# A two-layer hybrid trunk on one core: first token tile ahead of the norm scales, GpSimd makes the first weights' low part, squares added ahead of their sums, meta tokens' sums sent first

## Chip, core and metric

The kernel runs on one core of a Trainium2 chip. The metric is the device time of one execution in microseconds (us), lower is better. A profiled execution gives a trace beside it: a record for each instruction of TensorE (PE, with its weight loads as PEld), VectorE (DVE), ScalarE (ACT) and GpSimd (POOL), the issues of transfers by SyncE (SP), and the packets of the transfers.

## What is computed

Two layers over 528 tokens, 16 learned meta tokens ahead of 512, with a residual stream of 1024 channels. Each layer normalises the stream, projects it once into all inputs of two mixers (a causal pooling mixer, and latent attention with a rotary part and normalised queries and keys), gates both and adds the result:

```python
for l in range(DEPTH):
    h = rmsnorm(h_res, norm_gain[l])
    proj = h @ w_in[l]
    u_pool, z_pool, c_q, c_kv, k_rope, z_mla, g_pool, g_mla = jnp.split(proj, IN_SPLIT_POINTS, axis=-1)
    y_pool = (pool_mix(u_pool, pool_w_group[l], pool_scale[l]) * jax.nn.silu(z_pool)) @ pool_w_up[l]
    o_mla = mla(c_q, c_kv, k_rope, pos, ...)
    y_mla = (o_mla * jax.nn.silu(z_mla)) @ mla_w_up[l]
    merged = jax.nn.sigmoid(g_pool) * y_pool + jax.nn.sigmoid(g_mla) * y_mla
    h_res = h_res + merged @ w_out[l]
return h_res[:, N_META:]
```

Inside `mla` the latents `c_q` (768 wide) and `c_kv` (256 wide) have norms of their own; `q` and `k` of each of 8 heads (64 channels without and 32 with rotation) are normalised over their 96 channels. All in float32.

## The kernel before, in words

**Layout and products.** Activations lie transposed, channels on the 128 partitions and 528 tokens along the free axis. The stream is in eight tiles `xb[0..7]`, 128 channels each. Every big product is three products of the faster format fp32r: each operand is split into a high and a low part, and `mm3` adds high x high (L205), high x low (L206) and low x high (L207) in one accumulator. Weights come in pieces of 128x512: `wload` takes the piece, ScalarE writes its high part (L200), VectorE the low part (L201). The stream's tiles are split in the same way, scaled by the layer's gain: `hh` by ScalarE (L371), `hl` by VectorE (L373). The row of 528 tokens is cut in two halves of 264 (`FULL`), since an accumulator holds 512.

**What sets the order.** `plan` lists the projections with their columns and their `evac`, the code that reads an accumulator when it is complete. `stream` walks the plan, loads each weight piece some steps ahead and yields a nominal time after each few products; `step` takes one such piece of work. The rest of the kernel (norm statistics, attention heads) is straight code that asks for filler between its parts: `fill_now(ns)` runs steps worth so many nominal ns, `fill` does so up to a due time (`FILL`), and `after(ns, fn)` runs `fn` when so much filler has passed (`BACK`, `LATE`). From the code written in this way a scheduler fixes each engine's instructions in one static order. `behind(a, b)` makes `a` wait for `b`, and `follow(a, b)` only orders them. Transfers are nearly all issued by SP, in its order.

**The start.** The first weight piece is loaded by ScalarE's queue (tile `rinv`), then SP issues the gains (`gn`), the first token tile `xb[0]`, a second weight piece and `xb[1]`. `first` is the load of `gn`; all other loads of the start (`other_loads`) wait for it. The low and high part of the first two pieces lie in wide tiles `th`. GpSimd meanwhile clears some tiles. TensorE multiplies nine tiles of ones (L157) until the first operands are there; its first real products read `hh`, `hl` and `th` into `S`.

**Norm statistics.** `square_x` has ScalarE square the tiles of the stream and GpSimd add them to pairs and to fours: two tiles remain (of layer 1; layer 0 takes the sums from row copies of the input instead). `row_sums`, for layer 0, loads the tokens by rows (`xrow`, and `mrow` for the meta tokens), in nine pieces; ScalarE squares each and adds along the row into `sx`. `norm_sums` runs products with a block of ones (L426) over the two tiles of the stream and the two tiles `csq` of squares of `c_kv`, 32 columns wide, side by side in the array by `tile_position`; it writes the sums to `nsr` in DRAM (L440, and from `sx` L404 and L405), reads them back in another shape (`nq`, L448), and VectorE computes the inverse roots (`newton`) for `rinv` and the scale of `c_kv`, by which every accumulator of the projections is scaled when it is read.

**Statistics of queries and keys.** `q_stat` squares each block of the queries as it leaves its accumulator: two blocks `r` with the rotary channels of four heads each, four blocks `p` with the other channels of two heads each. `stat` collects the squares, `stat_go` sends a product (L535) for each of them, in two halves, with a matrix of constants that selects the heads, and `qk_stats` follows with the inverse roots.

**Heads.** `head` computes scores, exponentials and their row sums `rs`; the blocks go out to DRAM (`pdr`) and return transposed to `attE`, in `back`, some filler later. The inverse row sums go by DRAM (`rdr`) to a broadcast `rb`, and `gate` multiplies them into the gate on GpSimd.

Of the kernel before, what the change touches and what calls it, by code (L numbers as in the profile page):

```python
# [27 lines left out]
H = 8  # L28
# [3 lines left out]
TWO_PI = 2.0 * math.pi  # L32
SWAP = [i ^ 16 for i in range(32)]
# [19 lines left out]
FILL = (2620.0, 2530.0)  # L53
# [27 lines left out]
def trunk(ctx, tc, xT, xrow, mrow, pos, win, wkr, wqb, wkb, wvb, wgr, wpu, wmu, wout, gains, const, yT):  # L81
# [60 lines left out]
    act.dma_start(early[0][:, 0:512], win[0, MT_CKV, :, 0:512])  # L142
    first = sp.dma_start(gn, gains)
    sp.dma_start(xb[:, 0, :T], xT[:, 0, :])
# [45 lines left out]
    loads = [0]  # L190

    def wload(src, n, spare, home=None):
        raw = early.pop(0) if early else fetch(src, n, rawt() if home is None else home, sp)
        loads[0] += 1
        if loads[0] <= 2 or spare:
            t = wide()
            hi, lo = t[:, 0:512], t[:, 512:1024]
        else:
            hi, lo = (wp.tile([P, 512], F32R, tag=t, name=nm(t), bufs=3) for t in ("whi", "wlo"))
        act.activation(hi[:, :n], raw[:, :n], AF.Copy)  # L200
        dve.tensor_sub(lo[:, :n], raw[:, :n], hi[:, :n].bitcast(F32))  # L201
        return hi, lo
# [135 lines left out]
    nsr = [dp.tile([4, T], F32, name=f"nsr{l}") for l in range(DEPTH)]  # L338
# [9 lines left out]
    class Layer:  # L348
        def __init__(self, l):
# [11 lines left out]
            self.sq, self.half = [], halves()  # L361
# [14 lines left out]
        def square_x(self, k):  # L376
            self.xsq[k] = slot(f"cq{4 + k}" if k < 4 else f"q{k}")
            made = act.activation(self.xsq[k][:, :T], self.xt[k][:, :T], AF.Square)
            for w in (1, 2):
# [4 lines left out]
        def row_sums(self):  # L384
            sx = sm.tile([P, 2, 5], F32, tag="sx", name=nm("sx"))
            tags = ("q4", "q5", "q6", "q7", "kn0", "kn1", "kn2", "bc", "bc")
            rows = []
            for i in range(2 * len(tags) + 4):
# [3 lines left out]
                if i % 2 == 0 and len(rows) < len(tags):  # L392
                    k = len(rows)
                    r, src = (P, xrow[:, k]) if k < 8 else (2 * NM, mrow)
                    rows.append(slot(tags[k], bufs=3 if tags[k] == "bc" else 1)[0:r, 0:512])
                    behind(sp.dma_start(rows[k], src), newest[0])
                if i % 2 == 1 and i >= 5:
                    k = (i - 5) // 2
                    t = rows[k]
                    made = act.activation(t, t, AF.Square, accum_out=sx[0:t.shape[0], k % 2, k // 2:k // 2 + 1])  # L400
                    behind(made, newest[0])
                yield
            raw = nsr[0]
            sp.dma_start(raw[0:2, NM:T].rearrange("h (p i) -> p h i", i=4), sx[:, :, 0:4])  # L404
            sp.dma_start(raw[0:2, 0:NM].rearrange("h m -> m h"), sx[0:2 * NM, 0, 4:5])  # L405

        def norm_sums(self):
# [10 lines left out]
            px, pc = mmt() if self.l else None, mmt()  # L418
            xs = self.xsq[::4] if self.l else []
            runs = [(px, t, m, m < 2, m >= len(xs) - 2) for m, t in enumerate(xs)]  # L420
            runs += [(pc, t, m, True, True) for m, t in enumerate(self.csq)]
            for k in range(0, len(runs), 2):
                for s, (a, b) in enumerate(FULL):
                    for ps, t, m, start, stop in runs[k:k + 2]:
                        g = 64 * s + 32 * (m % 2)
                        mm = pe.matmul(ps[g:g + 32, :HALF], ones[:, 0:32], t[:, a:b], start=start, stop=stop,  # L426
                                       tile_position=(0, g))
                        if t is not self.csq[1]:
                            behind(mm, self.csq_last)
            self.kr_sums()  # L430
            sums = tmp()
            for s, (a, b) in enumerate(FULL):
                if self.l:
                    act.activation(sums[0:64, a:b], px[64 * s:64 * s + 64, :HALF], AF.Copy)
                dve.tensor_copy(sums[64:128, a:b], pc[64 * s:64 * s + 64, :HALF])
            raw, norms = nsr[self.l], ndr[self.l]
            if self.l:
                sp.dma_start(raw, sums[0:97:32, 0:T])
            else:
                sp.dma_start(raw[2:4], sums[64:97:32, 0:T])  # L440
                for _ in rows:
# [4 lines left out]
            nq = sm.tile([16, 4, C], F32, tag="nq", name=nm("nq"))  # L446
# [3 lines left out]
            dve.scalar_tensor_tensor(out=na[:, 0, :], in0=nq[:, 1, :], scalar=1.0 / D, in1=na[:, 0, :],  # L450
                                     op0=ALU.mult, op1=ALU.add)
            dve.tensor_scalar(na[:, 1, :], na[:, 0, :], EPS, None, op0=ALU.mult)
            dve.tensor_scalar(ny[:, 2, :], na[:, 1, :], EPS, None, op0=ALU.mult)
            for m in range(2):
# [841 lines left out]
```

## Time and profile before

| | us |
|---|---|
| median of three runs | 756.11 |
| the runs | 755.23 to 756.22 |
| the profiled execution | 756.64 |
| its span, from the first to the last instruction | 754.9 |
| TensorE busy in it | 749.7 |
| VectorE, ScalarE, GpSimd busy | 548.1, 395.9, 218.8 |

The profiled execution lies 1.74 us above its own span; that part, ahead of and behind the instructions, has no records. A row of the timeline gives start and duration in us, engine, line, operation, written tile <- read tiles, shape and, in brackets, how long the engine had been idle before and what released it. Rows with an engine's name and a q are of its sequencer (issues of transfers, configuration). A row of the chain gives start, duration, engine, tile and line of a stretch on the chain that ended last. A row of waits gives the waiting line, what it waited for, and us in total, times, and the longest.

### The profile page before, as it was taken

Reading aid. Unit: us, or ns where it says so; the run is one execution under the profiler, and the core shown is the slowest. Engines: PE = TensorE matmul, PEld = TensorE weight load, DVE = VectorE, ACT = ScalarE, POOL = GpSimd, SP = SyncE. Lnnn points to the kernel's source line nnn. Section 1 sums busy time; section 2 is a strip of 40 time slices with the busy share of each in tenths; the row PEclk is TensorE's granted clock in tenths of the full one; section 3 lists DMA queues with packets and bytes.
Section 4 is the critical chain, followed back from the end, with each engine's and each line's share of the span. In section 5 each row is a group of like instructions: output and inputs, shape, how many; then the busy total and the mean of one; then the engine's idle time right before and its main releaser. Section 6 shows DMA issues by size and latency. Waiting matters only on the chain.

```text
span 754.9 us, 14329 instructions
## 1 busy us (share of the span) xinstructions
PE 749.7 (99%) x5038; PEld 682.9 (90%) x5038; DVE 548.1 (73%) x1209; ACT 395.9 (52%) x866; POOL 218.8 (29%) x267
## 2 busy tenths in 40 slices
PE   9999999999999999999999999999999999999998
PEld 8999899999999999999997898887788888888887
DVE  5588777457999988684466477676478999975942
ACT  6755655645565665542355446456345666653321
POOL 1126404204463620061130264023044435111400
PEclk9999999999999999999999999999999999999999
DMA  8532223443765567525642322234447756773472
GB/s 316 162 108 89 74 82 86 113 116 119 211 186 166 151 194 192 156 86 157 183 145 85 114 84 66 89 90 120 108 135 210 190 156 181 195 200 93 127 227 84
DMA packets 72853, 106.58 MB, mean 141 GB/s; under 512 B 14102, under 2 KB 34966, under 8 KB 72780
## 3 DMA queue, kind: packets, MB, share of 16 engines
q1 hardware_dynamic: 72636, 105.39, 47.6%
q8 instruction: 40, 0.66, 0.4%
q14 instruction: 33, 0.27, 0.1%
q10 hardware_dynamic: 144, 0.26, 0.1%
HBM read 89.76 MB, written 15.86 MB: 140 GB/s over the span
## 4 chain that ended last, share of the span: by engine, by line
PE 98%; DMA 1%; ACT 0%; SPq 0%; issue 0%; DVE 0%; ACTq 0%
PE mm L205 29%; PE mm L207 29%; PE mm L206 29%; PE S L205 2%; PE S L207 2%; PE S L206 2%; PE o L980 1%; PE o L983 1%; PE S L535 1%; PE S L881 1%; DMA attE<-pdr 1%; PE S L501 0%; DMA xb<-xT 0%; PE mm L995 0%; PE mm L426 0%
## 5 line engine op out<-in xcount | busy, mean ns | idle before, releaser
L205 PE MATMUL mm<-hh,whi 128*128 128x264 f32 (+2 forms) x1072 | 336.1, 315 | 0.6 <-ACT whi L200 0.6
L206 PE MATMUL mm<-hl,whi 128*128 128x264 f32 (+2 forms) x1072 | 336.6, 315 | 0.0
L207 PE MATMUL mm<-hh,wlo 128*128 128x264 f32 (+2 forms) x1072 | 336.4, 316 | 0.0
L201 DVE TENSOR_TENSOR wlo<-raw,whi 128x512 fp32r<-128x512 f32 (+2 forms) x238 | 173.4, 730 | 95.8 <-ACT whi L200 92.4
L200 ACT ACTIVATE whi<-raw 128x512 fp32r<-128x512 f32 (+2 forms) x238 | 142.3, 600 | 176.1 <-PE mm L206 136.4
L205 PEld LDWEIGHTS mm<-hh,whi 128*128 128x128 f32 x1072 | 201.3, 188 | 15.0 <-issue 0.8
L206 PEld LDWEIGHTS mm<-hl,whi 128*128 128x128 f32 x1072 | 201.6, 188 | 12.9
L207 PEld LDWEIGHTS mm<-hh,wlo 128*128 128x128 f32 x1072 | 200.9, 188 | 12.3
L649 POOL TENSOR_TENSOR racc<-racc,tmp 128x264 f32<-128x264 f32 (+1 forms) x15 | 14.4, 959 | 132.3 <-ACT tmp L648 132.3
L1055 POOL TENSOR_TENSOR tmp<-tmp,xb 128x264 f32<-128x264 f32 (+1 forms) x24 | 27.0, 1137 | 49.1 <-DVE tmp L1053 46.4
L833 DVE CUSTOM_DVE_ANT_0 S<-S,maskw,nqs 128x240 f32<-128x240 f32 (+4 forms) x80 | 37.8, 492 | 4.2 <-PE S L207 3.9
L811 POOL CAST qhl<-q 32x528 fp32r<-32x528 f32 (+1 forms) x32 | 25.1, 800 | 44.2 <-PE S L881 42.9
L809 POOL CAST kh<-cq 32x528 fp32r<-32x528 f32 x16 | 15.6, 976 | 69.8 <-issue 36.1
L206 PE MATMUL mm<-th,whi 128*128 128x264 f32 (+1 forms) x108 | 34.7, 321 | 0.0
L205 PE MATMUL mm<-cq,whi 128*128 128x264 f32 (+1 forms) x108 | 34.7, 321 | 0.0
L205 PE MATMUL mm<-u,whi 128*128 128x264 f32 (+1 forms) x108 | 34.6, 321 | 0.0
L206 PE MATMUL mm<-cq,whi 128*128 128x264 f32 (+1 forms) x108 | 34.5, 321 | 0.0
L207 PE MATMUL mm<-cq,wlo 128*128 128x264 f32 (+1 forms) x108 | 34.5, 321 | 0.0
L207 PE MATMUL mm<-u,wlo 128*128 128x264 f32 (+1 forms) x108 | 34.5, 319 | 0.0
L959 DVE TENSOR_TENSOR attE<-attE,th 128x640 fp32r<-128x640 f32 x32 | 26.9, 862 | 3.7 <-ACT th L958 3.7
L840 ACT ACTIVATE cq<-S,bia 128x400 f32<-128x400 f32 (+2 forms) x48 | 24.4, 511 | 9.2 <-DVE bia L894 7.7
L843 POOL COPY pm<-cq 128x16 f32<-128x16 f32 x32 | 18.2, 570 | 37.7 <-ACT cq L840 37.5
(301 smaller groups left out, 1369.5 us busy)
## 6 DMA issues: line engine op xcount, KB each, us to landing
raw<-win SPq DMA_DIRECT2D x143, 256.0 KB, 3.2
pdr<-attD SPq DMA_DIRECT2D x16, 640.0 KB, 3.7
attE<-pdr SPq DMA_DIRECT2D x64, 160.0 KB, 3.9
raw<-wout SPq DMA_DIRECT2D x32, 256.0 KB, 2.8
raw<-wpu SPq DMA_DIRECT2D x16, 256.0 KB, 2.7
raw<-wmu SPq DMA_DIRECT2D x16, 256.0 KB, 2.7
raw<-wqb SPq DMA_DIRECT2D x12, 256.0 KB, 2.6
xb<-xT SPq DMA_DIRECT2D x8, 264.0 KB, 5.5
```

Source lines behind the costliest of these rows:

```text
L200: act.activation(hi[:, :n], raw[:, :n], AF.Copy)
L201: dve.tensor_sub(lo[:, :n], raw[:, :n], hi[:, :n].bitcast(F32))
L205: first = pe.matmul(out, wh, xh, start=start, stop=False)
L206: pe.matmul(out, wh, xl, start=False, stop=False)
L207: newest[0] = pe.matmul(out, wl, xh, start=False, stop=stop)
L809: gp.tensor_copy(d[r0:r0 + 32, :], f[g0:g0 + 32, :])
L811: gp.tensor_copy(d[r0:r0 + 32, x0:T], f[g0:g0 + 32, x0:T])
L833: return dve.tensor_tensor_reduce(out=sv, in0=sv, in1=mask, scale=nqs[:, i, h:h + 1], scalar=3e38, op0=ALU.add, op1=ALU.min, accum_out=bia ...
L840: act.activation(pv, sv, AF.Exp, scale=-1.0, bias=bia[:, i:i + 1], accum_out=rs[:, c:c + 1])
L843: gp.tensor_copy(pm[:, i, 16 * odd:16 * odd + 16], pt[i][:, 0:NM])
L959: dve.tensor_sub(got[:, a:b], f[:, a:b], hi[:, a:b].bitcast(F32))
L1055: gp.tensor_add(t[:, :b - a], t[:, :b - a], self.am[m][:, a:b])
```

## The change

In the order of the code:

- `SEAT` gives the heads of one rotary block another order, so that the rotary squares of two heads lie on the partitions on which the squares of their other channels are added.
- SP issues `xb[0]` ahead of `gn`. The other loads of the start still wait for `gn`.
- `wload` has the low part of the first piece made by GpSimd. The v weights' loads, so far issued as early as the scheduler could, wait for an earlier weight piece.
- `square_x` goes on to one tile; GpSimd adds the two `csq` tiles; `norm_sums` multiplies one tile of each. `nsr` and `nq` become one row smaller for each.
- `row_sums` takes the meta tokens first and writes their sums as soon as they are there; the other sums follow behind.
- `q_stat` keeps the squares of the rotary blocks (`rsq`) and has them added onto the squares of the other channels, by GpSimd for p = 0 to 2 and VectorE for p = 3, 32 partitions at a time; the products for the rotary squares go. `qk_stats` asks for more filler ahead of them.
- In `head` the transfer of the inverse row sums goes out behind the reads of the blocks, and its broadcast follows a third of `BACK` later; the last gate comes at `BACK`.
- `FILL` is shorter; the first up-projection piece `mu1` of layer 0 takes ordinary tiles.

```diff
-FILL = (2620.0, 2530.0)
+FILL = (2583.0, 2493.0)
...
     act.dma_start(early[0][:, 0:512], win[0, MT_CKV, :, 0:512])
+    sp.dma_start(xb[:, 0, :T], xT[:, 0, :])
     first = sp.dma_start(gn, gains)
-    sp.dma_start(xb[:, 0, :T], xT[:, 0, :])
...
     def wload(src, n, spare, home=None):
-        raw = early.pop(0) if early else fetch(src, n, rawt() if home is None else home, sp)
+        if home is not None:
+            raw = home
+            behind(sp.dma_start(raw, src), marks[-4])
+        else:
+            raw = early.pop(0) if early else fetch(src, n, rawt(), sp)
         loads[0] += 1
+        marks.append(newest[0])
...
         act.activation(hi[:, :n], raw[:, :n], AF.Copy)
-        dve.tensor_sub(lo[:, :n], raw[:, :n], hi[:, :n].bitcast(F32))
+        (gp if loads[0] == 1 else dve).tensor_sub(lo[:, :n], raw[:, :n], hi[:, :n].bitcast(F32))
...
-            for w in (1, 2):
+            for w in (1, 2, 4):
...
-                    r, src = (P, xrow[:, k]) if k < 8 else (2 * NM, mrow)
+                    r, src = (P, xrow[:, k - 1]) if k else (2 * NM, mrow)
...
+                    if k == 0:
+                        meta = sp.dma_start(raw[0:2, 0:NM].rearrange("h m -> m h"), sx[0:2 * NM, 0, 4:5])
                 yield
-            raw = nsr[0]
-            sp.dma_start(raw[0:2, NM:T].rearrange("h (p i) -> p h i", i=4), sx[:, :, 0:4])
-            sp.dma_start(raw[0:2, 0:NM].rearrange("h m -> m h"), sx[0:2 * NM, 0, 4:5])
+            follow(sp.dma_start(raw[0:2, NM:T].rearrange("h (p i) -> p h i", i=4), sx[:, :, 0:4]), meta)
...
-            px, pc = mmt() if self.l else None, mmt()
-            xs = self.xsq[::4] if self.l else []
...
+            ps, c = mmt(), self.csq[0]
+            self.csq_last = gp.tensor_add(c[:, :T], c[:, :T], self.csq[1][:, :T])
+            runs = [(self.xsq[0], 0)] * self.l + [(c, 32)]
+            for i, (a, b) in enumerate(FULL):
+                for t, m in runs:
+                    g = 64 * i + m
+                    mm = pe.matmul(ps[g:g + 32, :HALF], ones[:, 0:32], t[:, a:b], start=True, stop=True,
+                                   tile_position=(0, g))
+                    behind(mm, self.csq_last)
...
+                    if r is not None:
+                        self.rsq[r, a0] = q
+                        continue
+                    eng = dve if p == 3 else gp
+                    for g in (0, 64):
+                        g += 32 * (p % 2)
+                        made = eng.tensor_add(q[g:g + 32, :n], q[g:g + 32, :n], self.rsq[p // 2, a0][g:g + 32, :n])
+                    self.stat(q[:, :n], a0, b0, C_IK + 6 - 2 * p, made)
...
-            fill_now(LAG + 100)
+            fill_now(LAG + 700)
...
-            sp.dma_start(row.rearrange("a (p i) -> p (a i)", i=4), rs[:, 0:4])
...
+                follow(sp.dma_start(row.rearrange("a (p i) -> p (a i)", i=4), rs[:, 0:4]), read)
+                after(BACK / 3, sums)
+
+            def sums():
...
-                after(LATE, gate)
+                after(LATE if h + 1 < H else BACK, gate)
...
-                plan[-1].spare = m % 2 == 1
+                plan[-1].spare = m % 2 == 1 and l + m > 1
```

**Where instructions move.** Each row names a line, an operation, the written tile <- the read ones, and a shape. On GpSimd at the start of the program, before (`smeta` is the last tile it clears, `kn` the rotary key weights; ISA is a configuration of the engine):

```order
L583 MEMSET u_134_859 128x16
L583 MEMSET u_153_976 128x16
L583 MEMSET u_178_1094 128x16
L778 MEMSET smeta_2415 32x128
L493 ISA
L493 TENSOR_TENSOR kn_33_264<-kn_33_264,gn 128x256
```

and with the change (`th_160` holds both parts of the first weight piece, `rinv_78` is the piece as loaded):

```order
L586 MEMSET u_134_857 128x16
L586 MEMSET u_153_974 128x16
L586 MEMSET u_178_1092 128x16
L788 MEMSET smeta_2432 32x128
L207 ISA
L207 TENSOR_TENSOR th_160<-rinv_78,th_160 128x512
L496 TENSOR_TENSOR kn_33_264<-kn_33_264,gn 128x256
```

The low part stands between the configuration and `kn`, which was the first instruction behind it. On SP, from the last row pieces to the read of the norm sums, before:

```order
L396 DMA bc_440<-mrow 32x512
L135 DMA raw_601<-win 128x512
L440 DMA nsr_117<-tmp_474 2x528
L135 DMA raw_643<-win 128x512
L404 DMA nsr_117<-sx_257 128x2x4
L135 DMA raw_689<-win 128x512
L405 DMA nsr_117<-sx_257 16x2x1
L448 DMA nq_563<-nsr_117 16x4x33
```

and with the change:

```order
L402 DMA bc_441<-xrow 128x512
L136 DMA raw_641<-win 128x512
L442 DMA nsr_117<-tmp_474 1x528
L411 DMA nsr_117<-sx_257 128x2x4
L136 DMA raw_687<-win 128x512
L451 DMA nq_562<-nsr_117 16x3x33
```

The write of the meta tokens' sums (16x2x1) has gone from between the other sums and the read; it stands seven rows ahead of this piece. On GpSimd, with the last query blocks of layer 0, before:

```order
L575 TENSOR_TENSOR q_331_1889<-q_331_1889,tcos 128x264 x2
L576 TENSOR_TENSOR q_331_1889<-q_331_1889,tmp_1892 128x264
L576 TENSOR_TENSOR q_331_1889<-q_331_1889,tmp_1907 128x264
L809 COPY kh_2459<-cq_419_2453 32x528
L807 COPY kh_2459<-kh_2457 64x528
```

and with the change (`attD`, `attE` and `xb` hold the squares):

```order
L578 TENSOR_TENSOR q_331_1887<-q_331_1887,tcos 128x264 x2
L740 TENSOR_TENSOR attD_1958<-attD_1958,xb 32x264 x4
L579 TENSOR_TENSOR q_331_1887<-q_331_1887,tmp_1890 128x264
L740 TENSOR_TENSOR attD_1958<-attD_1958,xb 32x264 x2
L579 TENSOR_TENSOR q_331_1887<-q_331_1887,tmp_1905 128x264
L740 TENSOR_TENSOR attD_1958<-attD_1958,xb 32x264 x2
L740 TENSOR_TENSOR attE_2077<-attE_2077,xb 32x264 x4
L819 COPY kh_2476<-cq_419_2470 32x528
```

Twelve additions now stand between and behind the rotation of the queries, ahead of the copies for the heads.

More of the change, by code (lines that the diff above doesn't have):

```diff
@@ L337, in trunk @@
     scr = dp.tile([P, 8, SEQ], F32, name="scr")
-    nsr = [dp.tile([4, T], F32, name=f"nsr{l}") for l in range(DEPTH)]
+    nsr = [dp.tile([3 - l, T], F32, name=f"nsr{l}") for l in range(DEPTH)]
     ndr = [dp.tile([3, T], F32, name=f"ndr{l}") for l in range(DEPTH)]
@@ L386, in row_sums @@
             tags = ("q4", "q5", "q6", "q7", "kn0", "kn1", "kn2", "bc", "bc")
-            rows = []
+            rows, raw = [], nsr[0]
             for i in range(2 * len(tags) + 4):
@@ L1233, in constants @@
     c[64:128, C_IK + 15] = 1.0
-    for i in range(4):
-        c[32 * i:32 * i + 32, C_IR + 12 + i] = 1.0
     c[0:32, C_KPE:C_KPE + 8] = 1.0
@@ L1266, in arrange @@
     no, ro = np.arange(64), 64 + np.arange(32)
-    cols = np.concatenate([QK * h + ro for h in range(H)] + [QK * h + no for h in range(H)])
+    cols = np.concatenate([QK * (h - h % 4 + SEAT[h % 4]) + ro for h in range(H)] + [QK * h + no for h in range(H)])
     wqb = tiles(w_q_b[:, :, cols])
```

61 lines of the change are left out of this document (26 added, 35 removed).

## Prediction, made before the changed kernel ran

> **What bounds the kernel now.** I read the page first: the busy times and the chain of work that ended last. Then TensorE's list of waits.
>
> ```profile
> PE 749.7 (99%) x5038; PEld 682.9 (90%) x5038; DVE 548.1 (73%) x1209; ACT 395.9 (52%) x866; POOL 218.8 (29%) x267
> PE 98%; DMA 1%; ACT 0%; SPq 0%; issue 0%; DVE 0%; ACTq 0%
> PE wps L157 <- DVE na L764: 1.1, 1, 1.1
> PE mm L205 <- ACT whi L200: 0.6, 1, 0.6
> PE S L205 <- ACT hh L371: 0.2, 1, 0.2
> ```
>
> TensorE (PE) is busy for 749.7 of 754.9 us, and the chain is made of it. Its waits add up to 2 us, and only one of them, 0.6 us, lies in the middle of the program. So an edit gains only where it takes products away or ends one of these waits. It costs wherever it makes TensorE wait: products run in the order written, a late operand holds everything behind it, and nothing further on has slack to give the time back. The other engines matter by when they deliver.
>
> **Products taken away.** The chain in order of time gives start, duration, line and number of records; each product leaves two records (a weight load and a product).
>
> ```profile
> 13.46 0.24 PE S L205 x2
> 24.81 0.58 PE mm L426 x8
> 25.39 1.78 PE S L501 x32
> 149.32 2.80 PE S L535 x48
> 405.28 1.03 PE mm L426 x16
> 528.08 2.80 PE S L535 x46
> ```
>
> An ordinary product of 264 columns costs 0.12 us. The narrow products with ones go side by side: 16 of them (32 records) in 1.78 us, so a group of four costs 0.445 us. The query and key statistics (L535) fall from 24 to 20 products in each layer, six groups to five: 2 x 0.445 = **-0.89**. (2.80 / 6 = 0.47 agrees.) Layer 1's norm sums (L426) fall from 8 to 4, two groups to one: 1.03 becomes about 0.58, **-0.45**. Layer 0's fall from 4 to 2, but two side by side should last as long as four: **0**; gains down to -0.2 are the bound.
>
> **What pays for them on GpSimd.** The missing products become additions. Prices are the mean ns of groups of equal shape on GpSimd (POOL):
>
> ```profile
> L649 POOL TENSOR_TENSOR racc<-racc,tmp 128x264 f32<-128x264 f32 x10 | 7.9, 791 | 63.8 <-ACT tmp L648 63.8
> L649 POOL TENSOR_TENSOR racc<-racc,tmp 128x512 f32<-128x512 f32 x5 | 6.5, 1295 | 68.4 <-ACT tmp L648 68.4
> L576 POOL TENSOR_TENSOR kp<-kn,tmp 128x264 f32<-128x264 f32 x4 | 4.3, 1087 | 1.5 <-DVE tmp L574 1.3
> L382 POOL TENSOR_TENSOR q<-q,q 128x528 f32<-128x528 f32 x3 | 4.8, 1584 | 9.1 <-ACT q L378 9.1
> 514.34 1.71 POOL L811 CAST qhl<-q 32x512 fp32r<-32x512 f32 x2
> ```
>
> Each layer gets 12 additions of 32x264 on GpSimd (and 4 on VectorE). Width sets the price there, not partitions (264 columns 0.79 to 1.09, 528 columns 1.58), so I price each at 0.9, bounds 0.8 and 1.3. In layer 1 GpSimd is free from 514.34 + 1.71 = 516.05. By the order the statistics come some five wide products later than at 528.08, near 529, so 13 us are there for 12 additions: 1.09 each is the point at which they begin to hold TensorE; at 0.9 they end near 527. In layer 0 they stand among the rope's instructions on the same queue, with less to tell the limit by. Taken as 0. At 1.3 each layer 1 would lose 12 x 0.21 = 2.5, and layer 0 at most as much again. The added addition ahead of L426 (at most 1.58) has the 15 products, 1.8 us, by which the order now puts L426 later; 0 to +0.4, I take 0.
>
> **The one wait in the middle.** TensorE's row at 57.97 is the 0.6 us wait:
>
> ```profile
> 30.79 0.39 SPq L404 DMA_DIRECT2D nsr<-sx  x1
> 31.80 0.66 SPq L405 DMA_DIRECT2D nsr<-sx  x1
> SPq L448 <- DMA nsr<-sx: 3.4, 1, 3.4
> 38.62 0.17 DVE L449 TENSOR_SCALAR na<-nq 16x33 f32<-16x33 f32 x1 [4.70 <-DMA nq<-nsr]
> 57.06 0.28 PE L207 MATMUL mm<-kh,wlo 128*128 128x264 f32 x1
> 57.40 0.76 DVE L584 TENSOR_TENSOR u<-mm,rinv 128x264 f32<-128x264 f32 x2
> 57.97 0.36 PE L205 MATMUL mm<-hh,whi 128*128 128x264 f32 x1 [0.62 <-ACT whi L200]
> ```
>
> It is put down to `whi`, but the product before began at 57.06, a step of 0.91 instead of 0.12, and what ends just before is VectorE's (DVE) reading of accumulators, at 57.40: the product needs one of them freed. VectorE is late from a backlog that starts at 38.62 with the norm scales, which had waited for SyncE's (SP's) read `nq` behind the second of two small writes. That second write, the meta tokens' sums, was issued 31.80 - 30.79 = 1.01 us behind the first. The change sends it long before, and `nq` waits for one write alone: at least 1.01 earlier, more than the 0.79 that TensorE loses. I take all of it, **-0.79**; it could stay whole (0), as code around it moves too.
>
> **Attention.** The row broadcast moves behind the four block reads on SP's queue, and gates follow a third of a return time later. Head 6 of layer 0 is just in time now:
>
> ```profile
> 289.71 1.37 ACT L958 ACTIVATE th<-attE 128x640 fp32r<-128x640 f32 x2 [0.22 <-DMA attE<-pdr]
> ```
>
> ScalarE waits 0.22 for those blocks. The reads now pass ahead of the broadcast (gain), but fillers are cut to other sizes. **+0.3**, bounds 0 and +1.0.
>
> **What costs nothing.** VectorE loses one instruction of 0.7 and a few of 0.2 and gets 4 narrow additions a layer, beside which it has idle time (548.1 of 754.9 us busy). The v weights' loads (2 x 256 KB) leave the start and are wanted long after. The heads' seats permute columns of a weight ahead of the kernel. If one of these were not covered, it would cost its own length, under 1 us, which the range holds.
>
> **The start.** Here one instruction changes engine.
>
> ```profile
> 0.74 0.39 SPq L143 DMA_DIRECT2D gn<-gains  x1
> 1.19 0.41 SPq L144 DMA_DIRECT2D xb<-xT  x1
> 3.81 0.63 ACT L200 ACTIVATE th<-rinv 128x512 fp32r<-128x512 f32 x1 [1.15 <-DMA rinv<-win]
> 4.13 0.19 POOL L778 MEMSET smeta<- 32x128 f32 x1
> 4.47 0.69 DVE L201 TENSOR_TENSOR th<-rinv,th 128x512 fp32r<-128x512 f32 x1 [3.46 <-ACT th L200]
> 5.20 0.80 PE L205 MATMUL S<-hh,th 128*128 128x264 f32 x2 [0.24 <-ACT hh L371]
> 5.96 0.28 PE L207 MATMUL S<-hh,th 128*128 128x264 f32 x1
> L493 POOLq MODIFY_POOL_CONFIG  x2: 1/1/1, 4.3 to 4.3; - x2
> 19.66 0.62 POOL L493 TENSOR_TENSOR kn<-kn,gn 128x256 f32<-128x256 f32 x1 [15.33 <-DMA kn<-wkr]
> ```
>
> The low part takes VectorE 0.69 from 4.47 and is read by the fourth product, at 5.96. On GpSimd it would take 1.30 to 1.58 (rows of 512 and 528 columns above), so it would end at 5.8 to 6.1 if GpSimd began at once. The token tile, issued 0.45 earlier, can bring TensorE's first product forward by 0.2 at most: ScalarE is with the high part until 4.44, and `hh`, which the 5.20 row waits for, can't begin before. If that were all: **-0.1**, bounds -0.2 and +0.3.
>
> But GpSimd has run only memsets by then. Between the last memset and its first two-operand instruction its sequencer holds two configuration instructions, at 4.3; today that instruction waits for its data until 19.66, and whatever they set off is hidden. In the changed order they stand directly ahead of the low part. That they set something off shows in the transfers (last columns: granted clock, DMA share, GB/s):
>
> ```profile
> 4.00:6.00 2.00, 1.75 (x10) 1.35 (x9) 1.51 (x3) 1.81 (x5) 0.32 (x4) 1.00 1.04 392
> 6.00:7.00 1.00, 1.00 (x9) 0.90 (x9) 0.97 (x3) 1.00 (x3) 0.00 (x0) 1.00 0.95 247
> 7.00:8.00 1.00, 1.00 (x11) 1.00 (x10) 1.00 (x2) 0.33 (x1) 0.00 (x0) 1.00 1.04 318
> 8.00:9.00 1.00, 1.00 (x10) 1.00 (x10) 0.18 (x1) 0.25 (x1) 0.00 (x0) 1.00 0.98 291
> 9.00:10.00 1.00, 1.00 (x8) 0.81 (x7) 0.47 (x1) 1.00 (x2) 0.00 (x0) 1.00 0.95 319
> 10.00:12.00 2.00, 2.00 (x19) 2.00 (x18) 1.85 (x4) 1.76 (x4) 0.00 (x0) 1.00 1.04 389
> ```
>
> The engines are full throughout, yet from 6 to 10 us they deliver 247 + 318 + 291 + 319 = 1175 KB where 390 a microsecond would make 1560. About 385 KB were carried that no queue lists, between the configuration and 10 us. I read that as code fetched for GpSimd, ready near 10. Then the low part ends near 10.1 + 1.30 = 11.4, and TensorE, which can't pass its fourth product, stands from 5.96 to 11.4: **+5.4**. Bounds: ready at 9 (+4.3) and at 10.3 with the dearer 1.58 (+5.9).
>
> The Trainium skill (GPSIMD Engine Reference, 2.1 Instruction dispatch) says that the first call of a freshly loaded GpSimd kernel pays about 6 us, 5.95 measured from the configuration, with no instruction to be seen for it. By it the low part would start at 4.3 + 5.95 = 10.25 and the start would cost 5.6, an estimate; no run here shows it yet.
>
> After the stand the products may run slowly: the eighteen warm-up products kept the array occupied until it had settled,
>
> ```profile
> 1.05 3.91 PE L157 MATMUL wps<-ones 128*128 128x128 f32 x18 [1.05 <-DVE na L764]
> ```
>
> and half of 3.91, 2.0, is what is lost if the same length passes at half pace. Between 0 and +2.0 I take **+0.7**, as no row shows either.
>
> **The sum.** Without the start: -0.89 - 0.45 - 0.79 + 0.3 = -1.83. With the code fetch: -1.83 + 5.4 + 0.7 = +4.3, so the profiled execution would go from 756.64 (its span 754.9 and 1.74 around it) to 760.9. It lies 0.53 above the median of the runs, 756.11, so the median becomes 760.4.
>
> **The rivals.** *The fetch isn't in the way*: it is over sooner, goes on in the background, or the dip is the shape of the constants' rows. For it speaks that no row before shows an instruction waiting for a fetch; against it, that the dip lasts until 10. Then -1.83 - 0.1 = -1.9: 754.2. *The same, and the wait near 58 stays*, with 0.2 more in attention: 755.2. For it speaks that VectorE is busy for 73%, so that the time freed at 38.62 may fill again; against it the 1.01 us. *GpSimd's additions arrive late*, decided at 1.09 us each in layer 1: at 1.3 us in both layers +5.0 on the first rival, 759.2. Against it stand the 0.79 rows; for it the 1.09 row, which is exactly the limit.
>
> **How the numbers follow.** Fetch in the way 0.60, at 760.4, its own range 758.6 to 762.2 (756.11 with -1.83 + 4.3 + 0, and with -1.83 + 5.9 + 2.0). Not in the way 0.27, at 754.2. Wait stays 0.08. Late additions 0.05. A measurement here can't tell less than 0.2%, 1.5 us, from no change: faster is below 754.6, which is most of the first rival with its bounds, 0.26; slower above 757.6, the fetch and the late additions, 0.63; the rest 0.11. A range of 753.8 to 762.0 leaves out the best third of the first rival and the dearest end of the fetch, under 2 in 10.
>
> **What would show it.** The fetch: GpSimd's row of the low part starts near 10, not 4.5, and TensorE's fourth product follows it, near 11.5. If that row starts before 5, the forecast has failed and the first rival holds. The products: L535 and layer 1's L426 one group shorter in the chain. The wait near 58 gone, with `nq` read near 35. If TensorE has a new wait ahead of the statistics, naming GpSimd, the additions are late.

## The result, and the profile after

| | us | to the kernel before |
|---|---|---|
| before, 8 runs | 756.29 (755.23 to 757.16) | |
| changed, 8 runs | 758.28 (757.37 to 759.25) | 1.0023, 95% interval 1.0013 to 1.0032 |
| changed, profiled execution | 758.11, span 756.3 | before: 756.64, span 754.9 |

The kernel became slower, by 1.7 us going by the ratio; the forecast was 4.3. On two other chips the same kernel later stood at 1.0010 and 1.0011 (intervals 1.0001 to 1.0019 and 1.0002 to 1.0020), so 0.8 to 1.7 us is what there is to explain, and it hides a gain and a loss that are both larger.

The page's busy times and chain, and TensorE's waits, in the changed kernel:

```profile
PE 750.3 (99%) x5010; PEld 683.8 (90%) x5010; DVE 558.4 (74%) x1213; ACT 395.5 (52%) x864; POOL 243.9 (32%) x295
PE 95%; DVE 2%; DMA 2%; ACT 1%; issue 0%; POOL 0%; ACTq 0%; POOLq 0%; SPq 0%
PE mm L211 <- ACT whi L206: 0.8, 1, 0.8
PE S L211 <- ACT hh L377: 0.4, 1, 0.4
PE mm L211 <- ACT tmp L651: 0.3, 1, 0.3
PE S L212 <- DVE hl L379: 0.2, 1, 0.2
```

There are 28 records, 14 products, fewer (the plain products that went leave two TensorE records each, as the nine of ones leave 18; an ordinary one leaves one), and yet TensorE is busy for 0.6 us more: something made products slower. Off TensorE lie 5% of the chain, where it was 2%. The timeline of the start shows both (start and duration in us):

```profile
0.74 0.39 SPq L144 DMA_DIRECT2D xb<-xT  x1
...
1.18 0.42 SPq L145 DMA_DIRECT2D gn<-gains  x1
...
4.62 0.63 ACT L206 ACTIVATE th<-rinv 128x512 fp32r<-128x512 f32 x1 [1.96 <-DMA rinv<-win]
4.78 0.80 SPq L167 DMA_DIRECT2D xb<-xT  x2
5.15 0.91 ACT L377 ACTIVATE hh<-xb,gn 128x264 fp32r<-128x264 f32 x2
5.33 1.27 POOL L207 TENSOR_TENSOR th<-rinv,th 128x512 fp32r<-128x512 f32 x1 [1.02 <-ACT th L206]
5.69 1.61 DVE L379 SCALAR_TENSOR_TENSOR hl<-xb,gn,hh 128x264 fp32r<-128x264 f32 x2 [4.68 <-ACT hh L377]
5.71 0.99 PE L211 MATMUL S<-hh,th 128*128 128x264 f32 x2 [0.45 <-ACT hh L377]
...
6.94 0.59 PE L212 MATMUL S<-hl,th 128*128 128x264 f32 x1 [0.24 <-DVE hl L379]
...
7.33 0.42 PE L213 MATMUL S<-hh,th 128*128 128x264 f32 x1
...
8.43 0.42 PE L213 MATMUL S<-hh,th 128*128 128x264 f32 x1
...
8.65 0.42 PE L212 MATMUL mm<-hl,th 128*128 128x264 f32 x1
...
11.15 0.29 PE L211 MATMUL mm<-hh,th 128*128 128x264 f32 x1
...
11.27 0.29 PE L212 MATMUL mm<-hl,th 128*128 128x264 f32 x1
```

Read it from the top. The tile now goes out first and the gains 0.44 us behind it. The first weights' high part begins at 4.62 instead of 3.81: their transfer shares the engines with the tile. The loads that wait for the gains go out at 4.78 instead of 3.48. GpSimd's low part begins at 5.33, which is 0.08 behind the end of the high part (4.62 + 0.63): nothing held it. While it runs, VectorE's two halves of `hl` take 1.61 us, where they took 0.90. TensorE's first product comes at 5.71 instead of 5.20, its third at 6.94 instead of 5.83. Then products follow at 0.22 us (8.43, 8.65) and only from 10.2 on at 0.12 (11.15, 11.27): the array works at half pace until then. The page's clock row reads full throughout; but the trace's records of the granted clock begin only at 10.12, with full clock, and the row says nothing of the time ahead of them.

Further on, the one wait of before has not gone in this profile; it has become two. The rows answer to those of the norm chain shown before:

```profile
35.49 0.39 SPq L411 DMA_DIRECT2D nsr<-sx  x1
...
41.36 0.17 DVE L452 TENSOR_SCALAR na<-nq 16x33 f32<-16x33 f32 x1 [3.10 <-DMA nq<-nsr]
...
53.37 0.28 PE L213 MATMUL mm<-hh,wlo 128*128 128x264 f32 x1
54.00 0.39 PE L211 MATMUL mm<-hh,whi 128*128 128x264 f32 x1 [0.34 <-ACT tmp L651]
...
60.03 0.28 PE L213 MATMUL mm<-kh,wlo 128*128 128x264 f32 x1
60.56 0.76 DVE L587 TENSOR_TENSOR u<-mm,rinv 128x264 f32<-128x264 f32 x2
...
61.13 0.36 PE L211 MATMUL mm<-hh,whi 128*128 128x264 f32 x1 [0.81 <-ACT whi L206]
```

TensorE loses 0.50 at 54.00 (a step of 0.63 instead of 0.12) and 0.98 at 61.13, 1.48 against 0.79 before. What was to be gained was gained, in the chain's rows for the statistics (L538, 20 products) and layer 1's norm sums (L430, 4):

```profile
153.60 2.35 PE S L538 x40
...
407.66 0.58 PE mm L430 x8
...
531.15 2.35 PE S L538 x38
```

2.35 instead of 2.80 twice, and 0.58 instead of 1.03: -1.35, as forecast. GpSimd's additions for layer 1's statistics were in time:

```profile
518.05 7.80 POOL L740 TENSOR_TENSOR attD<-attD,xb 32x248 f32<-32x248 f32 x8
525.93 3.69 POOL L740 TENSOR_TENSOR attE<-attE,xb 32x248 f32<-32x248 f32 x4
```

Twelve in 11.5 us, 0.96 each, ended at 529.6, ahead of the statistics at 531.15.

### The profile page after: what moved, and what is told of

It reads as the page before. It is cut to its first block, busy times and chain, and to the rows that moved or that the text cites. A ratio compares the mean times of both kernels' runs of the same rounds, so it can differ in the third digit from the quotient of the medians.

```text
span 756.3 us, 14316 instructions
## 1 busy us (share of the span) xinstructions
PE 750.3 (99%) x5010; PEld 683.8 (90%) x5010; DVE 558.4 (74%) x1213; ACT 395.5 (52%) x864; POOL 243.9 (32%) x295
## 4 chain that ended last, share of the span: by engine, by line
PE 95%; DVE 2%; DMA 2%; ACT 1%; issue 0%; POOL 0%; ACTq 0%; POOLq 0%; SPq 0%
PE mm L213 28%; PE mm L211 28%; PE mm L212 28%; PE S L212 2%; PE S L213 2%; PE S L211 2%; PE o L994 1%; PE o L997 1%; PE S L891 1%; PE S L538 1%; DMA rinv<-win 1%; PE S L504 0%; DMA nsr<-sx 0%; DVE wlo L207 0%; DMA nq<-nsr 0%
## 5 line engine op out<-in xcount | busy, mean ns | idle before, releaser
L207 DVE TENSOR_TENSOR wlo<-raw,whi 128x512 fp32r<-128x512 f32 (+2 forms) x239 | 178.8, 751 | 91.1 <-ACT whi L206 85.4
L821 POOL CAST qhl<-q 32x528 fp32r<-32x528 f32 (+1 forms) x32 | 27.5, 873 | 41.5 <-PE S L891 40.2
L938 POOL TENSOR_TENSOR u<-u,cq 128x512 f32<-128x512 f32 x8 | 13.5, 1690 | 64.0 <-DMA cq<-rdr 45.2
L850 ACT ACTIVATE cq<-S,bia 128x400 f32<-128x400 f32 (+2 forms) x48 | 24.4, 511 | 12.4 <-DVE bia L904 11.4
```

Source lines behind the costliest of these rows:

```text
L207: (gp if loads[0] == 1 else dve).tensor_sub(lo[:, :n], raw[:, :n], hi[:, :n].bitcast(F32))
L821: gp.tensor_copy(d[r0:r0 + 32, x0:T], f[gq:gq + 32, x0:T])
L850: act.activation(pv, sv, AF.Exp, scale=-1.0, bias=bia[:, i:i + 1], accum_out=rs[:, c:c + 1])
```

## The experiments

Times are medians. Ratios go to the kernel before, measured beside each of them on the same chip, where it stood at 755.3 to 755.8. Edits are made to the changed kernel where nothing else is said.

### Which edit of the start: one, the other, both, neither

e1 puts the low part back on VectorE:

```diff
-        (gp if loads[0] == 1 else dve).tensor_sub(lo[:, :n], raw[:, :n], hi[:, :n].bitcast(F32))
+        dve.tensor_sub(lo[:, :n], raw[:, :n], hi[:, :n].bitcast(F32))
```

e2 puts the gains first again:

```diff
-    sp.dma_start(xb[:, 0, :T], xT[:, 0, :])
     first = sp.dma_start(gn, gains)
+    sp.dma_start(xb[:, 0, :T], xT[:, 0, :])
```

e3 is the changed kernel with both of these, and e4 the kernel before with the reverse of both.

> The changed kernel with the first weights' low part back on VectorE; the first token tile still goes out ahead of the gains. Theory S (the start): GpSimd's low part ended at 6.60 us instead of 5.16, and while it ran VectorE's two halves of hl took 1.61 us instead of 0.90, so TensorE's third product came at 6.94; with it back on VectorE the third product follows the second by 0.2 to 0.4 us, and the kernel comes down by 0.5 to 1.0 from 758.3, to about 757.5; the first product still comes near 5.7, since the late first weights (high part at 4.62 instead of 3.81) are the order's doing. Rival M (the middle): the loss is made between 40 and 62 us, where the waits grew from 0.8 to 1.5 us, and the start is recovered later: 758.0 to 758.3. Fetch theory of the prediction: dead already if the row at 5.33 is right, since GpSimd began 0.08 us after the high part was there.

> The changed kernel with the gains again ahead of the first token tile; the low part stays on GpSimd. Theory S: the gains land near 3.5 us instead of 4.8, the loads behind them follow 1.3 us earlier, the first weights' high part starts near 3.8, TensorE's first product near 5.2; GpSimd's low part still holds VectorE's hl and TensorE's third or fourth product by 0.5 to 0.7 us. 757.2 to 757.6. Rival M: 758.0 to 758.3.

> The changed kernel with both edits of the start undone. Theory S: the start is that of the kernel before, and what is left is 1.3 us of products saved (less what the wait near 60 us has grown): 755.3 to 756.1. Rival M: 757.5 or more. Rival C (the array's rate is luck of its phase, and the edits of the start cost nothing by themselves): like the changed kernel, 758, in some executions.

> The kernel before with the two edits of the start alone. Theory S: 756.3 + 2.3 = 758.6, and a start as in the changed kernel (first product near 5.7, products 0.22 us apart until about 10 us). Rival M: 756.3, since no sum and no norm was moved. If the two edits cost less here than in the changed kernel, part of the cost comes with the later work.

| | us | ratio, interval |
|---|---|---|
| e1, tile first alone | 755.52 | 0.9999 (0.9990 to 1.0007) |
| e2, low part on GpSimd alone | 753.97 | 0.9977 (0.9968 to 0.9986) |
| e3, neither | 753.85 | 0.9977 (0.9968 to 0.9987) |
| e4, both, on the kernel before | 757.91 | 1.0033 (1.0023 to 1.0044) |

The start is the loss. Without its two edits the change is a gain of 1.7 us (e3: better than 755.3 to 756.1, which had left a part for the wait near 60), and the two edits alone make the kernel before 2.5 us slower. But by their ratios e1 came down by 1.8 us and e2 by 3.5 from the changed kernel, where 0.5 to 1.0 and 0.7 to 1.1 were expected, and the chips differ, so the parts had to be measured on one:

> The changed kernel, beside the three below on one chip: both edits of the start. Theory A (the edits add up): tile first 1.7, low part about 0, so both 1.7 above neither. Theory I (they add to more): 2.4 or more above neither, since the late start and the held-up hl together leave the array at half pace until 10 us in most executions.

> The token tile ahead of the gains, low part on VectorE. Both theories: 1.2 to 1.8 us above the kernel with neither edit, since the first weights land 0.5 to 0.8 us later, ScalarE has their high part and hh to do one after the other, and the loads behind the gains go out 1.1 us later.

> The low part on GpSimd, gains first. Theory A and I: 0 to 0.4 us above neither, GpSimd's row beginning within 0.1 us of the end of the high part. If it costs as much as both together less the tile, the edits simply add up.

> The changed kernel with the start of the kernel before: 0.9977 of the kernel before, as in its first timing, within 0.0007.

| | us | above neither |
|---|---|---|
| f1, both | 756.57 | 2.65 |
| f2, tile first alone | 755.54 | 1.62 |
| f3, low part on GpSimd alone | 754.15 | 0.23 |
| f4, neither | 753.92 (ratio 0.9980, 0.9972 to 0.9989) | |

Theory I by the medians: together they cost 2.65, where they would add up to 1.85. The excess of 0.8 is not clear of noise, since each ratio's interval is 0.7 us to either side. The profiles tell where the time goes. The same 168 products stand ahead of layer 0's norm products in all four kernels; the chain's rows of these for f4, f3, f2 and f1, from the top:

```profile
26.86 0.35 PE mm L430 x2
27.07 0.35 PE mm L430 x2
28.43 0.35 PE mm L430 x2
29.13 0.35 PE mm L430 x2
```

By 29 us f3 is 0.21 behind f4, f2 1.57 and f1 2.27, nearly all of what the four profiled executions differ by in the end (0.37, 1.67 and 2.62). Of f2's 1.57, 0.63 is the later first product (5.84 instead of 5.21); the rest is mostly eight more products at 0.22 instead of 0.12 us, the pace that is looked at below.

Alone, GpSimd's low part is nearly free, as the start of f3 shows:

```profile
3.76 0.63 ACT L206 ACTIVATE th<-rinv 128x512 fp32r<-128x512 f32 x1 [1.09 <-DMA rinv<-win]
...
4.47 1.27 POOL L207 TENSOR_TENSOR th<-rinv,th 128x512 fp32r<-128x512 f32 x1 [0.16 <-ACT th L206]
...
5.08 1.35 DVE L379 SCALAR_TENSOR_TENSOR hl<-xb,gn,hh 128x264 fp32r<-128x264 f32 x2 [4.07 <-ACT hh L377]
...
6.47 0.42 PE L213 MATMUL S<-hh,th 128*128 128x264 f32 x1
```

that of f4 beside it:

```profile
5.19 0.90 DVE L379 SCALAR_TENSOR_TENSOR hl<-xb,gn,hh 128x264 fp32r<-128x264 f32 x2
...
6.22 0.42 PE L213 MATMUL S<-hh,th 128*128 128x264 f32 x1
```

and, in f3's list of all that has the low part's line, GpSimd's configuration (count, shortest, middle and longest in ns, first and last start in us):

```profile
L207 POOLq MODIFY_POOL_CONFIG  x2: 1/1/1, 4.3 to 4.3; - x2
```

The configuration stands at 4.3 and the low part runs at 4.47, 0.08 behind the high part's end: there is no room for a fetch. It takes 1.27 instead of VectorE's 0.69 and makes `hl` longer, and the fourth product comes 0.25 later.

### What in the tile's order costs

e8 is e1 with the other loads gated by the tile:

```diff
-    sp.dma_start(xb[:, 0, :T], xT[:, 0, :])
-    first = sp.dma_start(gn, gains)
+    first = sp.dma_start(xb[:, 0, :T], xT[:, 0, :])
+    sp.dma_start(gn, gains)
```

> e1_low_dve (low part on VectorE, first token tile ahead of the gains) with the other loads of the start waiting for the tile instead of the gains. Theory G: the cost of the order is that the gains land behind the 264 KB tile (the waiting loads go out at 4.8 to 5.1 us instead of 3.5 to 3.9) and the transfer engines stand idle from 5 to 6.5 us; the tile lands little earlier than the gains there, so 0 to 0.5 us are won, 755.0 to 755.5. Rival H: the cost is in the first weights alone, whose transfer shares the engines with the tile (high part at 4.9 instead of 4.15): nothing is won.

755.77 us, ratio 1.0004 (0.9995 to 1.0013), beside e1's 0.9999 on another chip: nothing won, although the gated loads go out at 4.50 instead of e1's 5.08. The lateness of the loads behind the gains is not the main cost; the first weights' is, or the pace below. For the first weights the trace's packets show it. With the gains first (f4) the tile's packets begin at 3.05 us and the weights' are nearly done, the last of them starting at 3.35. With the tile first (f2) its packets begin at 1.77, beside the weights', and the high part, which waits for the weights, begins at 4.75 instead of 3.82.

### The pace of the array

e10 is the changed kernel, and g1 is f4, each with

```diff
-WARM = 9
+WARM = 11
```

> The changed kernel with eleven warm-up products of ones instead of nine, so that TensorE does not stand still between 5.26 and 5.71. Theory C: the array stays at half pace until 10.1 us in the changed kernel's profile because it stood still just then, 14 products of 0.22 instead of 0.12 us; with the gap filled the pace rises by 7 us and 1.0 to 1.4 us are won: 756.1 to 756.6. Rival D: what decides is where the window of the rate falls, by chance, or the wait for hl near 6.5 us, and the two products delay the first real one at half pace: 0 to +0.4.

> The changed kernel itself again, for its time beside these kernels on one chip and a second profile. If the waits near 54 and 61 us are the rule, they are there again (1.3 to 1.6 us in both), with a ratio of 1.002 to 1.003; if they were an accident of the first profile (transfers that moved 42 GB/s at 24 to 26 us), this profile lacks them and still the time is 2 us above the kernel before.

> The changed kernel with neither edit of the start and with eleven warm-up products instead of nine. In its profiles without them the first real product comes at 5.1 to 5.5 and the warm-up ends at 4.9 to 5.3. Theory C: the array reaches full pace earlier in the executions in which it now does so at 7 us; 0.2 to 0.6 us less than g2. Rival D: at half pace eleven products end at 5.7 and hold the first real one, 0.2 to 0.5 more than g2, in the same executions; the two cancel, equal within 0.2.

> The changed kernel with neither edit of the start once more, beside the longer warm-up: 0.9977 to 0.9982 of the kernel before.

| | us | ratio, interval |
|---|---|---|
| a2, the changed kernel | 756.38 | 1.0010 (1.0001 to 1.0019) |
| e10, with two more warm-up products | 755.28 | 1.0001 (0.9993 to 1.0010) |
| g2, neither edit | 753.72 | 0.9980 (0.9971 to 0.9989) |
| g1, with two more warm-up products | 754.11 | 0.9981 (0.9973 to 0.9990) |

On the changed kernel the two products win 1.1 us by the medians (the intervals overlap), where 1.0 to 1.4 was expected; on the kernel with neither edit, where the gap is shorter, they win nothing (0.4 worse by the medians, the same by the ratios). The eleven runs of a2 fall in two groups, three from 754.96 to 755.42 and eight from 756.23 to 756.66. In the profiles the half pace ends by 7.3 us in all ten executions in which the gains went first. Where the tile went first it lasted until 9.5 to 10.8 in six of ten, e1's among them, whose stretch from 8 to 9 us comes last here (the third number from the end is the granted clock, 1.00 being full pace):

```profile
7.05 0.29 PE L211 MATMUL mm<-hh,th 128*128 128x264 f32 x1
7.17 0.32 PE L212 MATMUL mm<-hl,th 128*128 128x264 f32 x1
...
7.73 0.42 PE L213 MATMUL S<-hh,th 128*128 128x264 f32 x1
7.95 0.42 PE L212 MATMUL mm<-hl,th 128*128 128x264 f32 x1
...
8.00:9.00 1.00, 1.00 (x6) 1.00 (x6) 0.79 (x2) 0.98 (x2) 0.00 (x0) 0.50 0.92 220
```

Here the array had full pace (0.12 from 7.05 to 7.17), lost it after TensorE had stood still for 1.3 us before its first product, and had it again at 10.7. Some 15 products at 0.22 instead of 0.12 are 1.5 us.

The edits alone do not decide it; when full clock is granted differs between executions. e8 has the tile first and TensorE stands for 1.0 us before its first product at 5.78, but full clock was granted at 4.13 and stayed, and its norm products come at 27.02, where e1 has them at 28.71. e10's own profile is of this kind, too: full clock at 4.52, before the added products had run. So that e10's gain comes through the pace is argued from the times, the distances and a2's two groups; no pair of profiles shows it.

### The waits near 54 and 61 us

In the profiles of a2 and f1 no step between products there is over 0.39 us; e10's has one of 1.00. So the 1.48 of the first profile is not the rule, and the first chip's 1.0023 beside 1.0010 may be just this. (For a profile without these waits a2 was expected to stay 2 us above the kernel before; it stood 0.8 above.) Three kernels have the norm chain earlier: e6 is the changed kernel, e7 is e3, e9 is e1, each with

```diff
-                for _ in range(8):
+                for _ in range(4):
                     step()
```

> The changed kernel, start untouched, with the loads and squares of the token rows begun four filler steps earlier, so that the last write of the sums comes some 2 us earlier against TensorE's products. Theory N: the changed kernel's late start costs twice, 2 us at the start itself and 1.5 to 2.2 us in the two waits near 54 and 61 us, since the norm chain then ends later against the products; here those two waits are gone, and the kernel comes down from 2.0 above the kernel before to about level with it (ratio 0.9995 to 1.0005, some 755.7). Rival M2: these waits have another cause (a buffer held by another engine), and the time stays near 1.0023.

> e3_start_back with the rows begun four steps earlier. There no wait over 0.39 us is left near 60 us, so by theory N nothing is gained: 753.6 to 754.1. Rival: if the rows' loads now delay the weights behind them on SP's queue, a new wait between 15 and 25 us, up to +1.

> e6_rows_early with the first weights' low part back on VectorE, the token tile still ahead of the gains. The low part cost 2.2 us between e1_low_dve and the changed kernel, but 0.1 between e3_start_back and e2_gn_first. Theory N: most of the 2.2 is the two waits near 54 and 61 us, tipped over by a start that is a little later still; here the waits are gone in both, so the low part is worth 0 to 0.5 us: ratio 0.9998 to 1.0005, 755.1 to 755.7. Rival L: the low part costs its 2 us at the start, through VectorE held up by GpSimd, whatever comes later: 0.9978 to 0.9985.

e6: 755.41 us, 1.0005 (0.9996 to 1.0014). Its profile has the slow start of the changed kernel (half pace until 10.3) and no wait over 0.1 near 60 us. But a2 and f1 lack the waits too, so this alone does not show the norm chain to be their cause. What speaks for it is the time from layer 0's norm products to the norm scales (the row of `na`): 12.5 us in the first profile, 11.5 in e10 and 12.7 in e11 below, which have a wait there, and 5.7 to 11.2 in the fifteen other profiles with the changed order, where no step there is over 0.39. What the waits cost on the average can't be told more closely than 0.4 to 1.4 us, since the changed kernel itself stands at 1.0010 or 1.0023. e7 missed: 754.90, 0.9996 (0.9988 to 1.0005), 1.4 us worse than e3. Its rival had the place, but not the way: TensorE has a new wait, 0.5 us at 24.4 us, and it is not for weights. ScalarE reads an accumulator there (L488, at 23.97) behind a square of the token rows (L406, 0.61 from 23.36):

```profile
PE mm L211 <- ACT q L488: 0.5, 1, 0.5
```

e9: 754.87, 0.9999 (0.9990 to 1.0008); by e6's 1.0005, on another chip, the low part is worth 0.5 us here, at the upper end of theory N and far from the 2 us of rival L; the intervals overlap.

### Is it worth sending the meta tokens' sums first?

e5 is e3 with the order of the kernel before:

```diff
-                    r, src = (P, xrow[:, k - 1]) if k else (2 * NM, mrow)
+                    r, src = (P, xrow[:, k]) if k < 8 else (2 * NM, mrow)
...
-                    if k == 0:
-                        meta = sp.dma_start(raw[0:2, 0:NM].rearrange("h m -> m h"), sx[0:2 * NM, 0, 4:5])
                 yield
...
+            sp.dma_start(raw[0:2, 0:NM].rearrange("h m -> m h"), sx[0:2 * NM, 0, 4:5])
```

and e11 is e5 with that order forced, `rest` and `meta` being the two writes:

```diff
+                    if k == 8:
+                        follow(made, last)
+                    last = made
...
+            follow(meta, rest)
```

> e3_start_back (the changed kernel with the start of the kernel before) with the meta tokens' sums last again, as in the kernel before, so two small writes stand ahead of the read of the norm sums. Theory P (as predicted): the order saves at least a microsecond ahead of nq, so without it the wait near 57 us comes back, +0.8: 754.6. Theory Q (slots): the token rows moved down one slot each when the meta rows took the first one, so the last write starts no earlier, and only the latency of the second write (4.1 instead of 3.1 us) is gained; the wait comes back in part, 0 to +0.5: 753.9 to 754.3.

> e5_meta_last did not have what it was made for: the scheduler squared the meta rows ahead of the last token rows, so their write still went first. Here the square and the write of the meta rows are forced behind the others, as in the kernel before; all else as e3_start_back. Theory P: the second write is worth about a microsecond at nq and with it the wait near 57 us (0.79): 754.0 to 754.6 if e3 is 753.5 in this batch. Rival Q: nq comes later, but the norm products now stand 15 products later too, and no wait returns: equal to e3 within 0.2.

e5: 753.72, 0.9982 (0.9974 to 0.9991), but it is no test: the scheduler sent the meta tokens' sums first all the same. e11: 754.29, 0.9987 (0.9978 to 0.9996), where e3 and its repeats stand at 0.9977 to 0.9980. In its profile the second write is back and so is a wait:

```profile
32.07 0.38 SPq L412 DMA_DIRECT2D nsr<-sx  x1
...
33.05 0.65 SPq L413 DMA_DIRECT2D nsr<-sx  x1
...
37.84 0.34 SPq L454 DMA_DIRECT2D nq<-nsr  x1
...
57.02 0.76 DVE L590 TENSOR_TENSOR u<-mm,rinv 128x264 f32<-128x264 f32 x2
...
57.59 0.36 PE L211 MATMUL mm<-hh,whi 128*128 128x264 f32 x1 [0.27 <-DVE u L590]
```

TensorE waits there (0.27 by the row, a step of 0.55 instead of 0.12), and e3 does not. This is as the mechanism forecast has it; the size is 0.5 to 0.75 by the ratios, whose intervals overlap, and the profiled execution is the slowest of its eleven (756.04), with other waits besides.

## Why the prediction was right in direction and wrong in size

**The direction: luck.** The kernel became slower, as forecast, but the term that was to make it so, a fetch of code, is nowhere to be seen. The measured 758.28 lies between the forecast's 760.4 and the first rival's 754.2, and is neither's.

**Products taken away: right.** -1.35 in the chain's rows against -1.34. Layer 0's two norm products cost what four did.

**GpSimd's additions: right.** 0.96 us each, priced at 0.9; the limit of 1.09 was close, 1.5 us in all.

**The wait in the middle: gone where the start is left alone.** e3 and f4 have no wait over 0.1 near 57, and with the second write put back part of it returns (e11). The step was to be that the norm scales come 1.01 earlier; they come at 37.17 in f4 and 38.24 in e3 instead of 38.62. Against the norm products, which the order now puts 15 products later, that is 10.3 and 11.1 us behind instead of 13.8, so the order has a share in it. In the changed kernel the wait grew to 1.48 in one profile and was gone in two; why is not shown. The prediction's bound "it could stay whole" did not hold that it could grow.

**Attention: +0.3 not seen, and the sum near by luck.** f4's waits name no head. The sum without the start was -1.83; e3, f4 and g2 measure -1.7, -1.5 and -1.5 (0.9977 to 0.9980 of 756). But without the +0.3 it would be -2.13, further off: 0.4 to 0.6 us of the products and the wait are not found again in the time, and no row here says where they went.

**The start: the step that failed.** The sentence was "I read that as code fetched for GpSimd, ready near 10. Then the low part ends near 10.1 + 1.30 = 11.4, and TensorE, which can't pass its fourth product, stands from 5.96 to 11.4: +5.4." The low part began at 5.33, and in f3 at 4.47, both 0.08 behind its input; the fourth product ran at 7.33. The step took a dip in the transfers for a fetch because it followed the configuration in time. The changed kernel speaks against it: the configuration stands at 4.3 again, GpSimd is at work from 5.33, and the dip is there, somewhat later, as the loads are:

```profile
8.00:9.00 1.00, 1.00 (x6) 1.00 (x6) 1.00 (x2) 1.00 (x2) 0.00 (x0) 1.00 0.99 297
9.00:10.00 1.00, 1.00 (x7) 1.00 (x6) 0.97 (x2) 0.57 (x2) 0.00 (x0) 1.00 1.04 273
12.00:14.00 2.00, 2.00 (x19) 2.00 (x18) 1.56 (x3) 1.96 (x4) 0.00 (x0) 1.00 1.03 383
```

The Trainium skill (GPSIMD Engine Reference, 2.1 Instruction dispatch) has some 6 us for the first call of a freshly loaded kernel. Nothing of this length is seen here: from configuration to first operation there are 0.2 us in f3, and the instruction was waiting for its data in them. Whether these configurations load anything, no run shows.

**What stood in its place.** The token tile's order, forecast at -0.1, costs 1.6 (f2 less f4): its transfer runs beside that of the first weights, so that ScalarE has their high part and `hh` to do one after the other when both are in, and TensorE starts some 0.6 later (5.84 in f2, 5.21 in f4). GpSimd's low part, alone 0.2, adds 1.0 to that (f1 less f2), by the medians. And the pace, forecast at +0.7 behind a stand of 5 us, stays at half or falls to it after a start that is half a microsecond late, in six of the ten profiles with the tile first: 0.8 of f2's 1.57 us, and 1.1 us by e10. The two edits make 2.65 where the forecast held 6.1 against them, and so 4.3 became 1.7 at most. The first rival was right that no fetch is in the way. Its 754.2 is what e2 and f3 measure, with the gains first and the low part on GpSimd (754.0 and 754.2); for the changed kernel it was off by 4, since it priced the tile's order at -0.1.

**A version that beats both** is the change without its two edits of the start: 0.9977 to 0.9980 of the kernel before on three chips.

**Open:** whether the two edits of the start cost more together than they add up to (0.8 by the medians, about 0.5 in the rows at 27 to 29 us; more products at half pace would do it, but too few profiles show it); what slows the transfers between 6 and 10 us.

## What to carry to other kernels

Ahead of the first product, ask of each transfer what it shares the engines with: a tile of 264 KB moved ahead of 24 KB by half a microsecond delayed the weights that no edit touched, and cost 1.6 us. When an engine that paces a kernel may lose its pace by standing still, a late start can be paid twice; keep it busy until its operands are there, and compare several executions, since one profile may show either pace. And a dip that follows an instruction in time isn't that instruction's doing until a second kernel moves the one without the other.

## What was not expected of the hardware

- The half pace of the array at the start shows in the distance of products (0.22 instead of 0.12), but not in the profile's granted clock as long as full clock has not been granted once: the row reads 1.00 there. A later fall is in the row: 0.50 from 8 to 9 us in e1. By the trace's records e1 has full clock from 3.88, half from 7.29 and full again from 10.70, 3.41 us apart both times; f1 has the same at 3.89, 7.30 and 10.72. The Trainium skill (TensorE: Matmul & The Clock Gate, Part 1) tells of half pace after an idle window of some 3.4 us and a window that runs freely. The times of e1 and f1 agree with such a window. But in e1 it was lost after a stretch in which TensorE had stood still for 1.3 us only; in e8, 1.0 us did not lose it.
- VectorE's `hl` takes longer while GpSimd works beside it: 0.90 us alone, 1.35 and 1.61 during GpSimd's low part, and both times it ended 0.7 us behind that.
- In the changed kernel's first profile the transfers moved 42 GB/s from 24 to 26 us at a share of 0.82, in the midst of the token rows' loads. In f1 and a2, the same kernel, it was 49 and 65, in the kernel before 243. No run here tells why.
